# Weight-sum preparation as a second class of side work, and wider steps between its additions

## Chip, cores and metric

The kernel runs on one core of one Trainium2 chip. The metric is the device time of one execution in microseconds (us). The core has a matrix engine (TensorE, PE in the profile; PEld is its weight load), a vector engine (VectorE, DVE), a scalar engine (ScalarE, ACT), a general engine (GpSimd, POOL) and a queue engine that issues most transfers (SyncE, SP). The matrix engine accumulates in PSUM banks; sixteen DMA engines carry all transfers, whichever queue they were issued on.

## What is computed

A trunk of two layers over 256 tokens of width 2048, float32. Each layer adds a token mixer and then a ConvGLU to the residual `h`:

```
h = x
h = h + mlstm_mixer(rmsnorm(h))      # layer 0: input projections, matrix memory in both directions, output projection
h = h + conv_glu(rmsnorm(h))
h = h + hgrn_mixer(rmsnorm(h))       # layer 1: gated linear recurrence in both directions, output projection
h = h + conv_glu(rmsnorm(h))
out = rmsnorm(h)

conv_glu(x): a, v = split(x @ w_up);  (gelu(conv3(a)) * v) @ w_down        # inner width 5504
```

## The kernel before

**Products.** Every weight is float32 and is split on the chip into a high and a low float32r part: ACT copies it to `wh` (L149), DVE subtracts to `wl` (L150); three products (high x high, high x low, low x high) are added in PSUM. The whole work is one list of chunks that `stream` walks through. A chunk is a matrix of 128 x 16 rows and 256 or 512 columns (`fm` with the features, `tm` with the tokens on the partitions), or a pair (`st`). Its raw weights come in loads of 1 MB into three buffers on SP's queue, in the order of the program (`late`, L375, and `load_raw`, L137); the splitting runs three pieces (of 0.5 MB) ahead of the products (`LOOK`).

**Pairs by seven products.** A pair computes 256 x 1024 outputs as 2 x 2 squares per two row tiles, in PSUM banks `pc`. For some of its units (`SEVEN` for the ConvGLU's down projections, `SEVEN_MIX` for a mixer's output projection) it uses seven products in place of eight, with sums of weight squares: T3 = B12 + B22, T1 = B12 + B11, T2 = B11 + T3, T4 = B21 + T2. At the end of the last such unit `mid` spreads the extra banks over the residual `hm`; its last two steps are `hm` additions on POOL (L562, L563). After the pair `done` adds the four `pc` banks (L568, DVE), and the norm's transposes (L414, PE) and squares (L508, ACT) follow.

**Where the sums come from.** For a mixer's pair DVE makes them on the spot (`combine`, L208). For the down projections of a ConvGLU they are prepared ahead into a DRAM scratch, `tscr`, and loaded with the weights (L199, L200). Of the 30 sums of a layer,

- 14 (`BY_TRANSFERS`) are made by transfers alone: `prepare_by_transfers` starts a `unit` every 28 us (`PERIOD`), not while a pair runs (`held`). A unit copies 1 MB from DRAM to DRAM on SP's queue (L375, `tscr<-in_w_d`); 12 us later POOL issues accumulating transfers (L590) that add 256 KB each: T3 and T1 (`tscr<-in_w_d`), then T2 and then T4 (`tscr<-tscr`), each 9 us behind the one before it. All keep the order of the program on their queue, and POOL waits at each for the data that it needs. The generator is started with the third chunk of layer 0's mixer and with the second of layer 1's.
- 16 are made by DVE during the ConvGLU's up projections (`prepare`): loads into `pwh` and `pwl`, four additions (L620), two stores (L623). It is started with the first up chunk of either half of the ConvGLU and begins 18 us later.

**The planner.** `Side` holds the generators that run beside the products: heads of the mixers, norm transposes, the two kinds of preparation. It has a clock of its own, `now`, that the product loops advance (`tick`: 0.65 for each row tile of an `fm` chunk, so 10.4 a chunk; 1.3 for a `tm` one, so 20.8; 0.65 for each product of a pair). A generator is stepped when its time has come; what it yields is the time until its next step. `until(ready)` steps all generators, due or not, again and again until a value is ready; `drain` does so until no generator is left. So the planner sets where in the program an instruction stands; on each engine the pinned ones keep that place, and the others are placed by the program's own estimate of time.

**The mixer's end.** `mixed` makes a mixer's output projection: chunk `c0` (512 columns), the pair `two` (1024), chunk `c3` (512). At the end of `c0`, `done` calls `side.drain()`, closes the mixer's memory and opens that of the pair. Then come `two`, `c3` and the ConvGLU: 22 up chunks, two pairs, 21 up chunks, two pairs. A pair of the ConvGLU begins, in `split_squares`, with a wait until all of its prepared sums have been issued (`ch.waits`).

Of the kernel before, what the change touches and what calls it, by code (L numbers as in the profile page):

```python
# [53 lines left out]
BY_TRANSFERS = 14  # L54
# [13 lines left out]
def trunk_kernel(ctx, tc, xT, x_d, fg_d, pp_d, cst_d, w_gate, w_first, w_aq, w_ak, w_av, w_ao, w_aout, w_ao2,  # L68
# [18 lines left out]
    def col(name, i):  # L87
        o = OFF[name] + i
        return pp[:, o:o + 1]
# [4 lines left out]

    class Side:
        def __init__(self):
            self.now, self.jobs = 0.0, []

        def push(self, gen):
            self.jobs.append([gen, self.now])  # L100

        def step(self, job):
            try:
                job[1] = self.now + (next(job[0]) or STEP)
            except StopIteration:
                self.jobs.remove(job)

        def tick(self, dt):
            self.now += dt
            for job in list(self.jobs):  # L110
                if job[1] <= self.now:
                    self.step(job)

        def until(self, ready):
            while not ready():
                assert self.jobs
                for job in list(self.jobs):
                    self.step(job)

        def drain(self):  # L120
# [2 lines left out]
    side, held = Side(), []  # L123
# [11 lines left out]
    def load_raw(src, b0, b1, start=nc.sync.dma_start):  # L135
        raw = wpool.tile([P, 2048], F32, tag="raw", bufs=RAW, name="raw")
        start(raw[:, :b1 - b0], src[:, b0:b1])  # L137
        return raw
# [46 lines left out]
    def temporary(pool_, name):  # L185
        return pool_.tile([P, 1536], F32, tag="avc", bufs=TEMP if pool_.name == "ff" else 2, name=name)

    def split_squares(ch, parts):

        units, raws, kept = (ch.nk + 1) // 2, {}, {}  # L190
        side.until(lambda: not ch.waits)

        def raw(u):
            if u not in raws and u < units:
                n = 1536 if u in ch.stored else min(2048, 1024 * ch.nk - 2048 * u)
                raws[u] = load_raw(ch.src, 2048 * u, 2048 * u + n)
                if u in ch.stored:
                    kept[u] = temporary(ch.pool, "T")
                    nc.sync.dma_start(kept[u], ch.stored[u][:, 0:1536])  # L199
                    nc.sync.dma_start(raws[u][:, 1536:2048], ch.stored[u][:, 1536:2048])  # L200
            return raws.get(u)

        def combine(u):
            r, T = raw(u), temporary(ch.pool, "T")
            B11, B22, B21, B12 = (r[:, j * 512:(j + 1) * 512] for j in range(4))
            T2, T3, T4 = (T[:, j * 512:(j + 1) * 512] for j in range(3))
            for x, y, out in ((B12, B22, T3), (B12, B11, B12), (B22, B12, T2), (B21, T2, T4)):
                dve.tensor_tensor(out, x, y, ALU.add)  # L208
            kept[u] = T

        for u in range(units):
            r = raw(u)
            yield *parts(r[:, 0:1024], 1024, more=ch.pool), 1
            if u + 1 in ch.seven and u + 1 not in ch.stored:
                combine(u + 1)
            if u in ch.seven:
                yield *parts(kept[u][:, 0:1024], 1024, more=ch.pool), 1
            if 2 * u + 1 < ch.nk:
                yield *parts(r[:, 1024:2048], 1024, more=ch.pool), 1
            if u in ch.seven:  # L220
                yield *parts(kept[u][:, 1024:1536], 512, more=ch.pool), 1
# [152 lines left out]
    def late(dst, src):  # L374
        tc.keep_in_program_order(nc.sync.dma_start(dst, src))  # L375
# [206 lines left out]
    def prepare_by_transfers(todo):  # L582

        def unit(src, dst, left):
            late(dst, src)
            T2, T3, T4, T1 = (dst[:, j * 512:(j + 1) * 512] for j in range(4))
            B11, B12 = src[:, 0:512], src[:, 1536:2048]
            yield 12.0
            for out, in_ in ((T3, B12), (T1, B11), (T2, T3), (T4, T2)):
                tc.keep_in_program_order(pool.dma_start(out, in_, accum_op=ALU.add))  # L590
                if out is not T3:
                    yield 9.0
            left.pop()

        for job in todo:
            while held:
                yield 1.0
            side.push(unit(*job))
            yield PERIOD

    def prepare(mp, todo, period):
# [534 lines left out]
    def ffn(layer, norm, nxt):  # L1136
        stack = ExitStack()
        box = dict(n=STORED * layer)
        chunks, pairs, todo = [], [], []

        def begin():
            box["mp"] = stack.enter_context(tc.tile_pool(name="ff", bufs=1))
            box["mp"].tile([P, LEAD], F32, name="lead")
            for ch in pairs:
                ch.pool = box["mp"]
            if isinstance(nxt, FinalNorm):
                nxt.begin(box["mp"])

        def done_up(f, i, GT, SX, seven):
            def go(ps):  # L1150
                mp, R = box["mp"], norm.R
                avc = temporary(mp, "avc")
                a, v, c = (avc[:, j * T:(j + 1) * T] for j in range(3))
                for z, p in ((a, ps[0]), (v, ps[1])):
                    act.copy(z, p[:, T:2 * T])  # L1155
                    dve.tensor_tensor(z, p[:, 0:T], z, ALU.add)  # L1156
                av = avc[:, 0:2 * T].rearrange("p (a b) -> p a b", a=2)
                dve.tensor_tensor(av, av, R.unsqueeze(1).broadcast_to([P, 2, T]), ALU.mult)
                cw = [col("conv_w", (layer * 3 + w) * FT + f) for w in range(3)]
                act.activation(c, a, AF.Identity, bias=col("conv_b", layer * FT + f), scale=cw[1])  # L1160
                dve.scalar_tensor_tensor(c[:, 1:T], a[:, 0:T - 1], cw[0], c[:, 1:T], ALU.mult, ALU.add)
                dve.scalar_tensor_tensor(c[:, 0:T - 1], a[:, 1:T], cw[2], c[:, 0:T - 1], ALU.mult, ALU.add)
                act.activation(c, c, AF.Gelu)
                dve.tensor_tensor(c, c, v, ALU.mult)
                g = slot(i, "g", mp)
                act.copy(g[:, 0:T], c)
                dve.tensor_tensor(g[:, T:2 * T], c, g[:, 0:T].bitcast(F32), ALU.subtract)
                GT.append(g)
                if i % 2 and i // 2 in seven:
                    n = seven.index(i // 2)  # L1170
                    z = GT[i - 1][:, P:T], GT[i - 1][:, T + P:2 * T]
                    SX[i // 2] = token_sums(mp, n, box["c"], c, avc[:, 0:2 * T], z)
                box["c"] = c
            return go

        for part, (f0, nf) in enumerate(((0, FA), (FA, FB))):
            GT, SX, seven = [], {}, SEVEN[part]

            def prep(part=part, nf=nf):
                if part == 0:  # L1180
                    begin()
                jobs = todo[BY_TRANSFERS:][0:FIRST] if part == 0 else todo[BY_TRANSFERS + FIRST:]
                side.push(prepare(box["mp"], jobs, (nf * 10.4 - 26.0) / len(jobs)))

            for i in range(nf):
                chunks.append(Chunk("fm", w_up[layer, f0 + i], KT, norm.x, done_up(f0 + i, i, GT, SX, seven),
                                    prep if i == 0 else None,
                                    swap=(2,) if part and i == 0 else (3,) if f0 + i == 1 else (), paced=True))

            for c0, src in ((0, w_d0[layer][:, f0 * 1024:(f0 + nf) * 1024]), (2, w_d1[layer][:, f0 * 1024:(f0 + nf) * 1024])):  # L1190
                ch = pair(src, nf, c0, lambda k, GT=GT: GT[k], lambda u, SX=SX: SX[u], nxt if part else None, seven)
                ch.waits = []
                for u in seven:
                    if u != FLY:
                        ch.stored[u] = tscr[box["n"]]
                        ch.waits.append(True)
                        todo.append((src[:, 2048 * u:2048 * (u + 1)], tscr[box["n"]], ch.waits))
                        box["n"] += 1
                pairs.append(ch)
                chunks.append(ch)  # L1200
            if part and isinstance(nxt, FinalNorm):
                pairs[-2].before = nxt.load
                pairs[-1].bank = nxt.bank
        return chunks, stack.close, lambda: side.push(prepare_by_transfers(todo[:BY_TRANSFERS]))


    pool.memset(ones, 1.0)
# [8 lines left out]
    nf = FinalNorm()  # L1216
    chunks = mlstm(n0, n1)
# [111 lines left out]
```

## Time and profile before

| | |
|---|---|
| median of 3 runs | 2431.85 us (2425.56 to 2431.94) |
| profiled execution | 2423.3 us, span 2421.5 us |
| granted TensorE clock in it | 0.992 |
| busy: PE, DVE, ACT, POOL | 98%, 83%, 57%, 12% of the span |
| instructions | 38387 |
| DMA | 624.32 MB, mean 258 GB/s |
| q1 (issued by SP) | 588.49 MB, 69.2% of the DMA engines' time |
| q0 (issued by POOL) | 32.58 MB, 8.9% |

Layer 0's mixer runs to about 424 us, its ConvGLU to about 1118, layer 1's mixer to about 1715, its ConvGLU to the end. The profile gives for each engine how long it was busy; a row of 40 digits shows the busy tenths of 40 slices of 60.5 us. A wait is given as "engine line <- releaser: us in total, times, longest". Durations and waits are from one execution.

### The profile page before, as it was taken

What the parts mean: (1) busy time and instruction counts of PE and PEld (TensorE: products, weight loads), DVE (VectorE), ACT (ScalarE), POOL (GpSimd) and SP (SyncE); (2) the same over time, 40 slices, a digit from 0 to 9 for tenths busy, and PEclk for the clock granted to TensorE, in tenths of its full rate; (3) what the DMA queues carried; (4) which work ended last, traced back from release to release, by engine and by line L of the source; (5) the groups of instructions that cost most, each with busy time, mean ns of one, the idle gap of its engine ahead of it and who ended that gap; (6) DMA issues with size and microseconds to landing.
All of it is one profiled execution on the core that took longest, in us unless ns stands there. A gap on an engine that the chain in (4) does not pass through costs nothing.

```text
span 2421.5 us, 38387 instructions
## 1 busy us (share of the span) xinstructions
PE 2372.3 (98%) x14524; PEld 2022.9 (84%) x14524; DVE 2002.2 (83%) x3244; ACT 1392.3 (57%) x2201; POOL 291.8 (12%) x356
## 2 busy tenths in 40 slices
PE   9999987999999999999999999999999999999998
PEld 8888866888888888887888888888888888888876
DVE  7766656888889888897888888889788889888888
ACT  7655534555566555576555555555655567555565
POOL 0211022000000000000343434330000000000000
PEclk9999988999999999999999999999999999999999
DMA  8986898787788877786787877865778788777785
GB/s 301 268 245 227 253 264 224 269 278 269 268 335 278 279 257 252 245 322 227 224 244 212 244 229 231 238 199 191 240 270 275 265 301 333 275 257 257 248 319 200
DMA packets 123275, 624.32 MB, mean 258 GB/s; under 512 B 13889, under 2 KB 14401, under 8 KB 74705
## 3 DMA queue, kind: packets, MB, share of 16 engines
q1 hardware_dynamic: 105264, 588.49, 69.2%
q0 software_dynamic: 17248, 32.58, 8.9%
q8 instruction: 114, 1.87, 0.3%
q10 hardware_dynamic: 576, 0.79, 0.1%
q14 instruction: 73, 0.59, 0.1%
HBM read 586.09 MB, written 94.44 MB: 281 GB/s over the span
## 4 chain that ended last, share of the span: by engine, by line
PE 84%; DMA 6%; DVE 5%; issue 2%; POOL 1%; ACT 1%; SPq 0%; POOLq 0%; DVEq 0%; ACTq 0%
PE mm L337 35%; PE mm L341 18%; PE mm L353 11%; PE pc L236 10%; PE mm L236 7%; DMA tscr<-in_w_d 3%; DVE wl L150 2%; DMA tscr<-tscr 2%; DVE kq L1015 1%; DMA T<-tscr 1%; PE pn L816 1%; DMA raw<-in_w_d 1%; PE py L1073 1%; DVE QK L1035 1%; DVE QK L1036 0%
## 5 line engine op out<-in xcount | busy, mean ns | idle before, releaser
L337 PE MATMUL mm<-xt,wh 128*128 128x512 f32 x3776 | 1320.5, 396 | 3.5 <-DVE xt L360 3.1
L149 ACT CAST wh<-raw 128x1024 fp32r<-128x1024 f32 (+1 forms) x844 | 875.9, 1043 | 657.9 <-PE mm L337 380.4
L150 DVE TENSOR_TENSOR wl<-raw,wh 128x1024 fp32r<-128x1024 f32 (+1 forms) x844 | 1032.9, 1228 | 260.0 <-ACT wh L149 257.0
L341 PE MATMUL mm<-xt,wl 128*128 128x256 f32 x3776 | 1048.6, 279 | 0.0
L337 PEld LDWEIGHTS mm<-xt,wh 128*128 128x128 f32 x3776 | 706.8, 188 | 166.4 <-DVE xt L360 3.7
L341 PEld LDWEIGHTS mm<-xt,wl 128*128 128x128 f32 x3776 | 710.9, 188 | 4.5 <-issue 0.4
L353 PE MATMUL mm<-wh,xt 128*128 128x512 f32 x1024 | 320.3, 391 | 1.0 <-ACT xt L359 0.8
L236 PE MATMUL pc<-wh,g 128*128 128x512 f32 x696 | 238.0, 390 | 0.0
L353 PEld LDWEIGHTS mm<-wh,xt 128*128 128x128 f32 x1024 | 191.8, 188 | 40.8 <-ACT xt L359 1.3
L353 PE MATMUL mm<-wl,xt 128*128 128x512 f32 x512 | 198.7, 392 | 0.4 <-DVE wl L150 0.4
L236 PE MATMUL mm<-wh,sx 128*128 128x512 f32 x444 | 158.0, 392 | 0.5 <-ACT wh L149 0.5
L562 POOL TENSOR_TENSOR hm<-hm,u 128x512 f32<-128x512 f32 x10 | 15.1, 1505 | 1176.0 <-DVE u L561 1176.0
L236 PEld LDWEIGHTS pc<-wh,g 128*128 128x128 f32 x696 | 131.1, 188 | 27.5
L150 DVE TENSOR_TENSOR wl<-T,wh 128x1024 fp32r<-128x1024 f32 (+1 forms) x148 | 141.4, 966 | 13.4 <-ACT wh L149 13.1
L149 ACT CAST wh<-T 128x1024 fp32r<-128x1024 f32 (+1 forms) x148 | 122.5, 835 | 51.2 <-DMA T<-tscr 14.4
L236 PE MATMUL pc<-wl,g 128*128 128x512 f32 x348 | 135.7, 390 | 0.0
L1155 ACT COPY avc<-mm 128x256 f32<-128x256 f32 x172 | 64.1, 373 | 88.1 <-PE mm L341 88.1
L353 PEld LDWEIGHTS mm<-wl,xt 128*128 128x128 f32 x512 | 96.1, 188 | 20.2 <-DVE wl L150 1.2
L236 PEld LDWEIGHTS mm<-wh,sx 128*128 128x128 f32 x444 | 83.9, 189 | 18.3 <-ACT wh L149 0.9
L236 PE MATMUL mm<-wl,sx 128*128 128x512 f32 x222 | 87.3, 393 | 0.6 <-DVE wl L150 0.6
L1156 DVE TENSOR_TENSOR avc<-mm,avc 128x256 f32<-128x256 f32 x172 | 72.1, 419 | 13.9 <-ACT avc L1155 13.7
L1015 DVE COPY kq<-QK 128x256 f32<-128x256 f32 x224 | 76.4, 361 | 4.2 <-POOL QK L988 4.2
(241 smaller groups left out, 2435.1 us busy)
## 6 DMA issues: line engine op xcount, KB each, us to landing
raw<-in_w_up SPq DMA_DIRECT2D x172, 1024.0 KB, 5.1
raw<-in_w_bq SPq DMA_DIRECT2D x48, 1024.0 KB, 6.5
raw<-in_w_d SPq DMA_DIRECT2D x60, 768.0 KB, 5.7
T<-tscr SPq DMA_DIRECT2D x60, 768.0 KB, 7.3
tscr<-in_w_d SPq DMA_DIRECT2D x28, 1024.0 KB, 9.9
raw<-in_w_ao SPq DMA_DIRECT2D x24, 1024.0 KB, 8.5
raw<-in_w_d SPq DMA_DIRECT2D x24, 1024.0 KB, 6.8
pwh<-in_w_d SPq DMA_DIRECT2D x36, 512.0 KB, 6.5
```

The lines of the kernel that those rows point to most:

```text
L149: pin(act.copy(wh[:, :m], r))
L150: pin(dve.tensor_tensor(wl[:, :m], r, wh[:, :m].bitcast(F32), ALU.subtract))
L236: pe.matmul(ps, a, b, start=id(ps) not in begun, stop=stop and i == 2)
L337: pe.matmul(ps[f], wh[:, c:c + P], x, start=k + kk == 0, stop=False)
L341: pe.matmul(ps[f][:, 0:T], wl[:, c:c + P], x[:, 0:T], start=False, stop=k + kk == ch.nk - 1)
L353: pe.matmul(ps[t], x[:, a + t * P:a + (t + 1) * P], w[:, c], start=st and i == 0, stop=sp and i == 2)
L816: pe.matmul(pn[:, 0:258], w, v, start=(i == 0), stop=(i == len(parts) - 1))
L1015: dve.tensor_copy(m[:, j].rearrange("k (m p j) -> k m p j", p=2, j=h), blocks(z, h, 0, T))
L1035: dve.tensor_tensor(ka, ka, gview(G, n, 1, h), ALU.mult)
L1073: pe.matmul(py[:, c], AT[:, s if s == t else 2 + s], V[:, s, j * P:(j + 1) * P], start=(s == 0), stop=(s == 1))
L1155: act.copy(z, p[:, T:2 * T])
L1156: dve.tensor_tensor(z, p[:, 0:T], z, ALU.add)
```

## The change

`Side` gets a second list, `behind`. The two kinds of preparation are pushed there. `tick` steps both lists, as before; `until` steps the second one only where its new argument says so, which is the wait for a pair's prepared sums. `drain` goes on until the first list is empty and leaves the second one as it is. And a unit's later additions (T2 behind T3 and T1, T4 behind T2) stand 14 in place of 9 apart.

```diff
     class Side:
         def __init__(self):
-            self.now, self.jobs = 0.0, []
-
-        def push(self, gen):
-            self.jobs.append([gen, self.now])
+            self.now, self.jobs, self.behind = 0.0, [], []
+
+        def push(self, gen, behind=False):
+            (self.behind if behind else self.jobs).append([gen, self.now])
 
         def step(self, job):
             try:
                 job[1] = self.now + (next(job[0]) or STEP)
             except StopIteration:
-                self.jobs.remove(job)
+                (self.jobs if job in self.jobs else self.behind).remove(job)
 
         def tick(self, dt):
             self.now += dt
-            for job in list(self.jobs):
+            for job in self.jobs + self.behind:
                 if job[1] <= self.now:
                     self.step(job)
 
-        def until(self, ready):
+        def until(self, ready, behind=False):
             while not ready():
-                assert self.jobs
-                for job in list(self.jobs):
+                them = self.jobs + self.behind if behind else list(self.jobs)
+                assert them
+                for job in them:
                     self.step(job)
 
         def drain(self):
...
     def split_squares(ch, parts):
 
         units, raws, kept = (ch.nk + 1) // 2, {}, {}
-        side.until(lambda: not ch.waits)
+        side.until(lambda: not ch.waits, True)
...
             for out, in_ in ((T3, B12), (T1, B11), (T2, T3), (T4, T2)):
                 tc.keep_in_program_order(pool.dma_start(out, in_, accum_op=ALU.add))
                 if out is not T3:
-                    yield 9.0
+                    yield 14.0
             left.pop()
 
         for job in todo:
             while held:
                 yield 1.0
-            side.push(unit(*job))
+            side.push(unit(*job), True)
             yield PERIOD
...
-                side.push(prepare(box["mp"], jobs, (nf * 10.4 - 26.0) / len(jobs)))
+                side.push(prepare(box["mp"], jobs, (nf * 10.4 - 26.0) / len(jobs)), True)
...
-        return chunks, stack.close, lambda: side.push(prepare_by_transfers(todo[:BY_TRANSFERS]))
+        return chunks, stack.close, lambda: side.push(prepare_by_transfers(todo[:BY_TRANSFERS]), True)
```

## The prediction

> **What bounds the kernel now.** I read the page first: which engine is full, and where it is not.
>
> ```profile
> span 2421.5 us, 38387 instructions
> PE 2372.3 (98%) x14524; PEld 2022.9 (84%) x14524; DVE 2002.2 (83%) x3244; ACT 1392.3 (57%) x2201; POOL 291.8 (12%) x356
> PE   9999987999999999999999999999999999999998
> POOL 0211022000000000000343434330000000000000
> PEclk9999988999999999999999999999999999999999
> ```
>
> TensorE is busy for 2372 of 2421.5 us. The two digits under 9 in mid-row (slices 6 and 7, about 303 to 424 us) are the only place where more than a little can be won; the clock row dips there too, and POOL, nearly idle elsewhere in layer 0, has two 2s. So next the table of stretches (columns: stretch, length, busy time and count of PE, PEld, DVE, ACT, POOL, then granted clock, DMA share, GB/s), first by stage.
>
> ```profile
> 0.00:300.00 300.00, 296.61 (x1706) 251.25 (x1707) 207.37 (x377) 178.09 (x298) 39.30 (x65) 1.00 0.82 257
> 300.00:424.00 124.00, 99.92 (x424) 79.39 (x423) 75.35 (x117) 53.45 (x83) 27.07 (x32) 0.89 0.92 248
> 424.00:660.00 236.00, 236.00 (x1367) 206.50 (x1366) 200.70 (x327) 134.90 (x216) 0.71 (x1) 1.00 0.79 269
> 1126.00:1624.00 498.00, 494.17 (x4439) 424.03 (x4439) 430.11 (x871) 266.97 (x509) 186.23 (x230) 1.00 0.75 223
> 1648.00:1716.00 68.00, 68.00 (x314) 56.40 (x313) 62.05 (x91) 39.95 (x60) 3.54 (x2) 1.00 0.56 195
> ```
>
> 300 to 424 us is the end of layer 0's mixer (its output projection). PE is idle there for 124.0 - 99.9 = 24.1 us, half of all its idle time. The row 1648 to 1716 is the same code in layer 1 (`mixed` builds the same chunks): no idle time, clock 1.00. In finer steps:
>
> ```profile
> 330.00:340.00 10.00, 6.50 (x29) 5.07 (x27) 0.00 (x0) 0.00 (x0) 0.00 (x0) 1.00 1.01 262
> 340.00:350.00 10.00, 3.25 (x6) 1.63 (x6) 6.12 (x12) 4.06 (x4) 0.81 (x1) 0.51 0.92 276
> 390.00:400.00 10.00, 5.46 (x29) 4.21 (x27) 1.14 (x2) 1.05 (x1) 3.34 (x4) 0.91 1.05 293
> 400.00:410.00 10.00, 4.58 (x18) 3.87 (x19) 4.54 (x6) 4.07 (x10) 4.95 (x5) 0.57 0.65 98
> ```
>
> Two holes, and the waits of 296 to 470 us name what ended them, the SP and POOL rows in order of time what stood in front.
>
> ```profile
> DVE T L208 <- DMA raw<-in_w_ao: 18.8, 2, 15.9
> DVE hm L568 <- POOL hm L562: 13.5, 1, 13.5
> 266.80 0.50 SPq L375 DMA_DIRECT2D tscr<-in_w_d  x1
> 298.07 0.50 SPq L375 DMA_DIRECT2D tscr<-in_w_d  x1
> 311.08 3.37 SPq L375 DMA_DIRECT2D tscr<-in_w_d  x5
> 307.04 1.70 POOL L590 DMA_DIRECT2D tscr<-in_w_d  x2
> 402.54 0.81 POOL L590 DMA_DIRECT2D tscr<-tscr  x1 [0.20 <-issue]
> 403.09 1.55 POOL L562 TENSOR_TENSOR hm<-hm,u 128x512 f32<-128x512 f32 x1
> ```
>
> First hole: five copies of 1 MB go to SP's queue in one go, the projection's own weights (`raw<-in_w_ao`) stand behind them, and the splitting of weights waits 15.9 us. Second hole: POOL works through the additions of seven units from 307 to 403 us, each waiting for the one before to land; the residual additions L562 and L563 stand behind them, DVE L568 behind those (13.5 us), and the transposes behind that. Both come from one call: `side.drain()` in `mixed.done` steps every job until none is left, so the units that are not due yet are issued back to back.
>
> **The change part by part.** *What the drain still issues.* On the planner's clock (0.65 a matmul pair of an fm step, 1.3 of a tm step: 10.4 a fm chunk, 20.8 a tm chunk) the transfers begin with the third chunk, at 31.2, one unit every 28; `mixed.done` comes at 4 x 62.4 + 20.8 = 270.4. Units 0 to 8 are out by then (the last at about 256), units 9 to 13 are not: the row x5 above. With the change the drain steps the first class alone, which is empty there, so these five leave the stretch. Unit 8 keeps its three steps: first additions at 268, then 282 and 296. In `two` (270.4 to 310) no unit begins, because `held` is set; unit 9 starts at 311, units 10 to 13 at 339, 367, 395 and 423, and the last addition falls at 463. ConvGLU begins at 331 and its pairs after 22 chunks, at 560, far behind 463: the wait in `split_squares` finds every unit done and costs nothing.
>
> *The gain.* The stretch from `two`'s first product to ConvGLU's first, in layer 0 and in layer 1:
>
> ```profile
> 325.46 0.39 PE L236 MATMUL pc<-wh,ya 128*128 128x512 f32 x1
> 423.71 0.39 PE L337 MATMUL mm<-xt,wh 128*128 128x512 f32 x1
> 1648.02 0.39 PE L236 MATMUL pc<-wh,yb 128*128 128x512 f32 x1
> 1715.40 0.39 PE L337 MATMUL mm<-xt,wh 128*128 128x512 f32 x1
> ```
>
> 98.25 against 67.38 us: 30.9 us for the same products, 24 of idle time and the rest a lower clock behind it. I take all of it as gain. What is late next: POOL still has units 7 and 8 in front of L562, beginning at 307 (row above), six steps with some 7 us to each landing (6.0 and 7.2, rows below): over before 350, while L562 falls due near 360, in the last third of `two`. DMA adds unit 8's additions, the end of unit 7's and the start of unit 9 (16 us of work by the prices below) to the twin's share of 0.56 in 67 us: about 0.80, which ConvGLU bears (0.79) without idle time.
>
> *The price: the five units land in ConvGLU.* What a unit takes of the 16 DMA engines stands in the DMA view of 1126 to 1624 us (layer 1's mixer), and what ConvGLU takes already in that of 440 to 640:
>
> ```profile
> q1 hardware_dynamic: 13166, 95.94, 54.6%
> q0 software_dynamic: 7918, 14.42, 20.4%
> tscr<-in_w_d POOLq DMA_DIRECT2D x28, 256.0 KB, 7.2
> tscr<-tscr POOLq DMA_DIRECT2D x27, 256.0 KB, 6.0
> q1 hardware_dynamic: 9792, 54.53, 79.7%
> ```
>
> q0 is the additions: 20.4% of 498 us over 55 of them is 1.85 us each, 7.4 us a unit. q1: 54.6% of 498 us for 95.94 MB is 2.83 us a MB, 3.0 for a unit's copy. `prepare` begins 18 after ConvGLU, at 349; from there to 463 are 114 of the planner's us, 122 on the chip by the rows below (5.54 us a load, two loads a chunk of 10.4). Free on the engines: 20.3% of 122 = 24.8 us. Wanted: three copies (9.0) and the additions of four units (29.6). The excess is 13.8 us.
>
> ```profile
> L375 SPq DMA_DIRECT2D raw<-in_w_up x37: 327/328/333, 439.7 to 639.3; - x37
>   PE mm L337: 64.5, 51
> DMA to landing us min/median/max: 4.7/5.5/8.5
> ```
>
> Not all of it reaches TensorE. Three raw buffers, 36 x 5.54 us: a load is issued when a buffer comes free and used two loads later, 11.1 us, and it lands after 5.5, so 5.6 us are spare; ACT's casts wait for TensorE (64.5 us, 51 times), so split pieces of 2.8 us each are ready ahead, two of them safely. Cover 11 us. I take 13.8 - 11 = 3 us; the ends are 0 (cover holds, or engines do more than share 1.00, as 1.05 above) and 14. If the cover were gone, it costs the 14.
>
> By bytes it looks milder: ConvGLU's 274 GB/s (54.73 MB in 200 us) and a unit's 2.1 MB in 30 us (28 on the planner's clock) come to 344 GB/s. The Trainium skill, DMA: Bandwidth & Descriptors, section "Where 436 GB/s comes from", puts a core's limit at HBM at about 358 GB/s; by that rule nothing would be in excess and the term would be 0. The trace disagrees for these transfers: the additions take 101.6 us for 14.42 MB.
>
> *9 to 14 between additions, and `until` without the second class.* In layer 1 POOL waits for the additions' landings while its mixer's products stand behind them; wider steps should remove most of that:
>
> ```profile
> POOL tscr L590 <- DMA tscr<-in_w_d: 22.5, 9, 4.0
> POOL tscr L590 <- DMA tscr<-tscr: 13.6, 6, 5.0
> ```
>
> But TensorE is idle only 3.8 us of those 498, so at most that is won, and POOL order may shift as much the other way: -3.8 to +3.8, taken as 0. Layer 1's last unit starts at 10.4 + 364 of 437 and its last addition is at 415, ahead of the mixer's end. In layer 0's first 300 us TensorE misses 3.4 us, the start included: 0, with the same bounds. Other `until` calls find their values ready by the planner's times (R at 27 against 31, the last head's transposes at 257 against 265), so not stepping the second class there changes nothing. No instruction is added or removed.
>
> *Sum.* -30.9 + 3 + 0 = -28 us against the profiled execution's 2423.3 us (span 2421.5): 2395. The three timed runs lie at 2425.56 to 2431.94, median 2431.85, 8.5 above it; taking the same difference there: 2404. About 0.3% (7 us) is what a measurement can tell from no change.
>
> **The rivals.** *Congestion in ConvGLU takes much of it back (0.14).* For: 0.80 + 0.32 is 112% of the DMA engines for 122 us. Against: the cover, and additions that only start when the ones before have landed, so they cannot pile up. Excess fully paid, with fluctuation and some clock: 8 to 22 us back, 2409 to 2423; still faster.
>
> *Slower (0.06).* The same place, but the additions cost double when loads, stores of `prepare` and additions share the engines: 14.8 us a unit makes the excess 43 us, less 11 of cover 32; with the clock lost as in 300 to 424 us (30.9 us of time for 24.1 of idle, 1.28) it is 41 against 31: 10 us slower, 2442. It decides from 1.7 times the price on (12.6 us a unit). Against it: in the densest stretch there is, the price did not rise:
>
> ```profile
> q0 software_dynamic: 4032, 7.34, 38.4%
> ```
>
> That is 300 to 424 us, share 0.92: 47.6 us for seven units, 6.8 each. The clock matters to this rival: after 3.5 us without products (330 to 340) it fell to 0.51. The Trainium skill, TensorE: Matmul & The Clock Gate, section "What's actually happening", says the clock halves after an idle window of about 3.4 us; holes of one missing piece (under 2.8 us) would then cost only themselves, and this case would end level, at 2433, not slower. No row here shows such short holes.
>
> *It does not do what it says (0.07).* The program places POOL's instructions by its own estimate; if the additions of units 7 to 9 still stand in front of L562, or the copies still meet the weights, the holes stay in other sizes: within 7 us of before. Against it: only one unit, not seven, can then be queued.
>
> **How the numbers follow.** Forecast 0.73 (gain 20 to 36 us: 2396 to 2412, with the runs' own spread of 6 us), rivals 0.14, 0.06, 0.07. Faster by over 0.3%: 0.73 + 0.14 = 0.87, less 0.01 for the end of the first rival: 0.86; same 0.08; slower 0.06. The range 2392 to 2420 holds the forecast and most of the first rival.
>
> **What would show it.** In the changed profile: no x5 row on SP near 311 us; L562 starting near 360 us, released by DVE L561; the stretch of 98.25 us at 67 to 70; POOL additions spread to about 530 us; from 400 to 530 us a DMA share near 1.0, and PE's idle time there is the price (3 us here; over 30 means the second rival). PE idle in layer 1's mixer should stay under 8 us. A stretch still over 85 us would make the prediction wrong at its root.

## The result, and the profile after

After the change the kernel takes 2396.86 us (median of 4 runs, 2388.61 to 2399.01) against 2429.87 (2425.56 to 2431.94) before: the ratio is 0.986, with a 95% interval of 0.9832 to 0.9888. Two further sets of runs gave 0.9865 [0.9843, 0.9886] and 0.9842 [0.9822, 0.9863]. It is some 33 us faster; 28 were forecast.

The profiled execution took 2388.61 us. In the new kernel every line from 116 on stands one number higher than before. Its page, the same rows as before:

```profile
span 2386.8 us, 38389 instructions
PE 2364.5 (99%) x14524; PEld 2020.7 (85%) x14524; DVE 2001.0 (84%) x3244; ACT 1392.7 (58%) x2201; POOL 290.9 (12%) x356
PE   9999999999999999999999999999999999999998
POOL 0211011000000000001334333330000000000000
PEclk9999999999999999999999999999999999999999
```

The digits under 9 in slices 6 and 7 are gone from the PE and the clock rows. In layer 1 POOL's digits begin one slice earlier, since layer 1's mixer starts earlier (its first products were at about 1121 us, now at 1095). The table of stretches, with the end of layer 0's mixer first and the start of its ConvGLU behind it:

```profile
300.00:392.00 92.00, 90.33 (x406) 74.10 (x406) 74.12 (x114) 52.36 (x80) 14.06 (x15) 0.98 0.78 232
392.00:660.00 268.00, 267.24 (x1515) 233.74 (x1513) 219.99 (x357) 153.03 (x241) 15.55 (x19) 1.00 0.89 300
400.00:530.00 130.00, 129.24 (x746) 113.24 (x745) 105.45 (x173) 71.93 (x115) 14.02 (x17) 1.00 1.00 331
```

PE is idle for 1.7 us in the first row, where it was 24.1. The DMA engines, which before had a share of 0.79 in ConvGLU, are full from 400 to 530 us, and the matrix engine hardly notices: 0.8 us idle of 130. The first products of `two`, of the last chunk and of ConvGLU, in the timeline:

```profile
325.07 0.39 PE L237 MATMUL pc<-wh,ya 128*128 128x512 f32 x1
370.32 0.62 PE L354 MATMUL mm<-wh,ya 128*128 128x512 f32 x2
394.85 0.39 PE L338 MATMUL mm<-xt,wh 128*128 128x512 f32 x1
```

The stretch is 69.78 us long instead of 98.25: 45.25 in `two` (62.13 before), 24.53 in the last chunk (36.11 before; 24.53 is also its length in layer 1). POOL and SP in order of time, and the wait that is left of the first hole:

```profile
302.38 0.71 POOL L514 TENSOR_TENSOR rs<-rs,mhalf 128x2 f32<-128x2 f32 x1 [42.97 <-DVE rs L513]
338.39 0.81 POOL L591 DMA_DIRECT2D tscr<-tscr  x1 [4.47 <-DMA tscr<-tscr]
371.68 1.29 POOL L563 TENSOR_TENSOR hm<-hm,u 128x512 f32<-128x512 f32 x1 [32.48 <-DVE u L562]
376.27 1.69 POOL L591 DMA_DIRECT2D tscr<-in_w_d  x2 [1.06 <-DMA tscr<-in_w_d]
510.19 0.81 POOL L591 DMA_DIRECT2D tscr<-tscr  x1 [8.80 <-DMA tscr<-tscr]
```

```profile
297.68 0.50 SPq L376 DMA_DIRECT2D tscr<-in_w_d  x1
305.81 45.60 SPq L138 DMA_DIRECT2D raw<-in_w_ao  x8
369.06 0.50 SPq L376 DMA_DIRECT2D tscr<-in_w_d  x1
392.33 0.50 SPq L376 DMA_DIRECT2D tscr<-in_w_d  x1
```

```profile
DVE T L209 <- DMA raw<-in_w_ao: 4.1, 2, 2.6
```

SP goes from a single copy (297.68) to the projection's own weights (305.81); no copy follows until 369. POOL has been idle for 32.48 us when the residual addition L563 (L562 before) comes due, and DVE releases it, not a landing. The last addition is issued at 510.

The whole execution by stages, each the distance between first products in the timeline (start of the program, of `two`, of the last chunk, of ConvGLU, of its first pairs; layer 1's mixer is counted from ConvGLU's last product, and the last pairs up to the end); two more profiled executions of the new kernel and one more of the old one stand beside them:

| stage, us | before | before, 2nd | after | after, 2nd | after, 3rd |
|---|---|---|---|---|---|
| start up to `two`, layer 0 | 325.46 | 327.63 | 325.07 | 326.32 | 331.43 |
| `two`, layer 0 | 62.13 | 63.27 | 45.25 | 47.46 | 46.19 |
| last chunk, layer 0 | 36.11 | 36.97 | 24.53 | 24.53 | 24.53 |
| ConvGLU's first up stage, layer 0 | 245.57 | 245.57 | 246.97 | 253.31 | 251.00 |
| layer 1's mixer up to the output projection | 505.02 | 505.63 | 500.02 | 500.46 | 501.89 |
| last pairs to the end | 120.09 | 116.23 | 116.62 | 118.01 | 116.68 |

In the main profile the stages give -28.5, +1.4, -5.0 and -3.5 us, all others together +0.9: -34.7, the difference of the spans. The -3.5 of the last pairs is not the change's: the second execution of before has 116.23 there as well. The third execution of after begins `two` late, because TensorE once waited 5.39 us near 98 us; E7 below has a like wait.

### The profile page after: what moved, and what is told of

It reads as the page before. It is cut to its first block, busy times and chain, and to the rows that moved or that the text cites. A ratio compares the mean times of both kernels' runs of the same rounds, so it can differ in the third digit from the quotient of the medians.

```text
span 2386.8 us, 38389 instructions
## 1 busy us (share of the span) xinstructions
PE 2364.5 (99%) x14524; PEld 2020.7 (85%) x14524; DVE 2001.0 (84%) x3244; ACT 1392.7 (58%) x2201; POOL 290.9 (12%) x356
## 4 chain that ended last, share of the span: by engine, by line
PE 87%; DMA 5%; DVE 5%; issue 1%; ACT 1%; POOL 0%; SPq 0%; DVEq 0%; POOLq 0%; ACTq 0%
PE mm L338 34%; PE mm L342 17%; PE mm L354 14%; PE pc L237 11%; PE mm L237 7%; DVE wl L151 2%; DMA raw<-in_w_up 1%; DMA T<-tscr 1%; PE pn L817 1%; DMA tscr<-in_w_d 1%; DMA raw<-in_w_ao 1%; PE py L1074 1%; DMA raw<-in_w_d 1%; DMA pwh<-in_w_d 1%; ACT wh L150 0%
## 5 line engine op out<-in xcount | busy, mean ns | idle before, releaser
L563 POOL TENSOR_TENSOR hm<-hm,u 128x512 f32<-128x512 f32 x10 | 15.7, 1566 | 1094.7 <-DVE u L562 1094.7
L237 PEld LDWEIGHTS pc<-wl,g 128*128 128x128 f32 x348 | 65.3, 188 | 13.9 <-DVE wl L151 0.6
```

What stands on the lines that cost most here:

```text
L237: pe.matmul(ps, a, b, start=id(ps) not in begun, stop=stop and i == 2)
L563: pool.tensor_tensor(part(1, 0), part(1, 0), u, ALU.add)
```

## The experiments

Theory: two holes with two causes (copies ahead of the projection's weights on SP; additions ahead of the residual additions on POOL), both out of the one `drain`; the wider spacing is worth nothing. Rivals: the spacing carries the gain, or one cause carries both holes, or the price in ConvGLU is hidden or much larger.

**E1, the spacing alone.** The kernel before, with

```diff
-                    yield 9.0
+                    yield 14.0
```

> The kernel before, with the additions of a unit 14 in place of 9 apart and one class of side work: the drain still issues five units back to back. My theory (the gain is the drain's burst alone): both holes between 300 and 424 us stay, about 98 us from the pair's first product to ConvGLU's first, time within 0.3% of before; layer 1's mixer may be up to 4 us shorter, which is the whole effect of the spacing. Rival (POOL's waits for landings cost time all over, and the spacing takes them away): 10 us or more faster, the second hole smaller.

Ratio 1.0011 [0.9999, 1.0024], 2431.1 against 2428.22 us: no gain. Both holes stay: `two` is 66.24 us long, the last chunk 35.64.

**E2, the classes alone.** The kernel after, with the spacing back:

```diff
-                    yield 14.0
+                    yield 9.0
```

> The changed kernel with the additions 9 apart as before: only the two classes. My theory: the stretch at 68 to 71 us, the whole gain, ratio to before 0.985 to 0.989, layer 1's mixer as before. Rival (spacing shares in it): 0.990 or more, with POOL additions standing in front of the residual additions, or more idle TensorE time in ConvGLU.

0.9891 [0.9873, 0.9909], 2402.04 us. `two` is 44.91, the last chunk 24.53: both holes are gone. The classes carry the gain. Layer 1's mixer is at 505.48, as before. Within the classes only `drain` acts: with `until` stepping both lists, as it did, and `drain` the first alone, the program has the same instructions in the same order on all five engines as E2.

**The kernel after once more,** in the same set:

> The changed kernel as it is, beside the others on one chip. Both theories: ratio 0.983 to 0.989. It shows how much of the 4.3 us that layer 1's mixer and of the 3.5 us that the last pairs were shorter in the first profile comes back: if they do, the spacing has a share; if they do not, they were that execution's.

0.9865 [0.9843, 0.9886], 2399.88 us. Its ratio and E2's overlap, so that the timing alone doesn't tell the spacing from nothing. Of the two differences that it was to show again, that of layer 1's mixer is back in full (500.46), that of the last pairs in part (118.01).

**E4, the second cause taken away by itself.** The kernel before, with the residual additions on DVE, away from POOL's queue:

```diff
-            pool.tensor_tensor(part(1, 0), part(1, 0), u, ALU.add)
-            pool.tensor_tensor(part(1, 1), part(1, 1), u, ALU.subtract)
+            dve.tensor_tensor(part(1, 0), part(1, 0), u, ALU.add)
+            dve.tensor_tensor(part(1, 1), part(1, 1), u, ALU.subtract)
```

> The kernel before, with the last two residual additions of a pair's middle on DVE in place of POOL; the drain and its burst stay. My theory (two holes with two causes, SP's queue and POOL's queue): the second hole (10 us idle and the clock behind it) goes, the first stays; the stretch 84 to 88 us, 10 to 14 us faster, ratio 0.994 to 0.996. Rival (one cause, the DMA engines full of the units): the second hole stays or only moves, within 0.3% of before.

0.9983 [0.9973, 0.9993], 2425.15 against 2428.22 us. The second hole is gone and the first untouched: the last chunk is 24.53, `two` 62.32. So there are two causes. But of the 11.6 us won there the time shows only 3. In the profiles they are lost in ConvGLU, where nothing waits: its first up stage in layer 0 and both up stages in layer 1 take 249.93, 249.93 and 237.55 us instead of 245.57, 245.57 and 233.18, 13.1 us together. The groups of layer 1's first up stage (columns: count, busy, mean ns), in E4 and in before:

```profile
L337 PE MATMUL mm<-xt,wh 128*128 128x512 f32 x683 | 241.4, 399 | 0.0
```

```profile
L337 PE MATMUL mm<-xt,wh 128*128 128x512 f32 x686 | 238.2, 394 | 0.0
```

The same products, no idle time in front of either, and 399 in place of 394 ns for one. As far as the profiles show, the size that E4 was to give failed on this, not on the hole. They are one execution each, and E4's is 3.1 us longer than before's while its median is 3.1 shorter, so that the sizes fit only roughly.

**E5, the first cause put back by itself.** The kernel after, where all copies that are left are issued at the end of the mixer's first output chunk, and the additions keep their new times:

```diff
+        copied = []
+
+        def copy(job):
+            if job not in copied:
+                copied.append(job)
+                late(job[1], job[0])
+
+        rests.append(lambda: [copy(job) for job in todo])
...
+            for rest in rests:
+                rest()
```

> The changed kernel, but at the end of the mixer's first output chunk the copies of all units that have not begun are issued at once on SP's queue (their additions stay spread). My theory (the first hole is SP's queue: five copies of 3 us each in front of the pair's weights): the hole near 340 us is back, the pair 52 to 60 us in place of 45 to 47, no second hole, 7 to 14 us slower than the changed kernel, ratio to before 0.989 to 0.993. Rival (the first hole was the additions' traffic on the DMA engines): the pair at 45 to 48 us, as fast as the changed kernel.

0.9954 [0.9938, 0.9969], 2418.36 against 2429.45 us. SP's row, the wait and the stretches of E5:

```profile
311.54 3.71 SPq L376 DMA_DIRECT2D tscr<-in_w_d  x5
```

```profile
DVE T L209 <- DMA raw<-in_w_ao: 18.0, 2, 17.8
```

```profile
330.00:340.00 10.00, 6.97 (x31) 5.44 (x29) 0.00 (x0) 0.00 (x0) 1.68 (x2) 1.00 1.01 287
340.00:350.00 10.00, 1.37 (x2) 0.79 (x3) 3.72 (x8) 2.09 (x2) 0.81 (x1) 0.55 1.02 294
```

The five copies on SP alone make the whole first hole, 12 us without products at the same place as before; `two` is 61.30 against 42.85 in layer 1, the last chunk stays at 24.53. It is the larger of the two holes: of the 33 us, E5 leaves 11. That is 22 us lost, and not the 7 to 14 expected. `two` is 14 to 16 us longer than in the three executions of the kernel after. The profiled execution (2410.18 us) was the fastest of nine, 8 us under their median, so that no profile shows where the rest goes.

**E6, the price in ConvGLU.** The kernel after, with the last five units not before ConvGLU and twice as close:

```diff
-        for job in todo:
-            while held:
+        for k, job in enumerate(todo):
+            while held or (k >= 9 and side.now < 350.0):
                 yield 1.0
             side.push(unit(*job), True)
-            yield PERIOD
+            yield 14.0 if 349.0 < side.now < 600.0 else PERIOD
```

> The changed kernel, but layer 0's last five units begin only when ConvGLU's own preparation has begun (350 on the planner's clock) and then 14 apart: five units of 10.4 us of DMA time in 103 us of which 21 are free. By my arithmetic the excess is 31 us, less 11 of cover: 20 us slower than the changed kernel, ConvGLU's first up stage about 265 us, ratio to before about 0.994 to 0.996. Rival (the DMA engines or the cover have more room than I gave them): less than 8 us slower, ratio 0.987 to 0.990.

0.9907 [0.9881, 0.9933], 2407.14 us. ConvGLU's first up stage takes 255.99 us, 10.4 over before. One stretch of E6, then the landings of the weights' loads from 440 to 520 us in E6, then those in after:

```profile
440.00:520.00 80.00, 73.39 (x404) 62.27 (x403) 59.10 (x97) 39.58 (x64) 12.81 (x16) 0.98 1.04 339
```

```profile
DMA to landing us min/median/max: 7.3/14.6/18.8
```

```profile
DMA to landing us min/median/max: 6.7/10.1/16.5
```

Here the cover of 11.1 us between a load's issue and its use is over (median 14.6), and PE stands idle for 6.6 of 80 us. In the kernel after, the median lies just under it. A price exists and grows with the density, but less steeply than the excess that I had worked out: the dense case loses 10, not 20. The ratio lies between what my theory and what its rival gave.

**E7 and E8, where the units before the drain go.** The kernel after, with units 18 or 22 apart (in place of 28) in the first 300 us of the planner's clock, so that fewer are left for later:

```diff
-            yield PERIOD
+            yield 18.0 if side.now < 300.0 else PERIOD
```

```diff
-            yield PERIOD
+            yield 22.0 if side.now < 300.0 else PERIOD
```

> The changed kernel with units 18 in place of 28 apart in layer 0's mixer, so that all 14 begin before its first output chunk ends and none is left for ConvGLU. My theory: POOL has the additions of four units between the last heads' scales (306 us) and the residual additions, some eight landings of 7 us, to about 365 us, just when those fall due, and DMA has 40 us of work in the pair on top of its own 0.56: the pair 48 to 56 us, ConvGLU's first up stage at 245.6 us; 0 to 8 us slower than the changed kernel. Rival (what ConvGLU pays is the larger part): 2 to 5 us faster than the changed kernel.

> The changed kernel with units 22 apart in layer 0's mixer: eleven begin there, three are left for ConvGLU, and POOL has two units between the scales and the residual additions as in the changed kernel. My theory: the pair at 45 to 47 us as there, ConvGLU's first up stage free of stalls: 0 to 4 us faster than the changed kernel, ratio to before 0.984 to 0.987. Rival (the mixer's heads wait behind more additions on POOL): slower than the changed kernel, with idle TensorE time before 300 us.

E7: 0.9892 [0.9872, 0.9913], 2403.68 us. ConvGLU's first stage is free of any price (245.57), but `two` takes 51.50: more additions now fall due while POOL waits in front of `two`, they are issued from 315 to 354 us, and the projection's weights come late again. One copy on SP's queue (319.21 us) also stands between the projection's loads. `two` begins late, too, at 333.59 us: 5.65 us of that is one wait of TensorE at 97.7 us, and since the third execution of after has a like one, it isn't shown to belong to E7. A wait and the hole in PE's timeline of E7:

```profile
DVE T L209 <- DMA raw<-in_w_ao: 8.1, 2, 4.2
```

```profile
363.08 0.80 PE L237 MATMUL pc<-wh,ya 128*128 128x512 f32 x1 [5.75 <-ACT wh L150]
```

E8: 0.9849 [0.9826, 0.9872], 2392.99 us; `two` is 44.00, ConvGLU's first stage 246.32. Run again beside the kernel after:

> The changed kernel with units 22 apart in layer 0's mixer, again, beside the changed kernel on the same chip. If moving two units out of ConvGLU is worth what the profiles show (1 us in the pair, 1 to 7 in ConvGLU's first up stage): 2 to 6 us faster than the changed kernel. If not: within 1 us.

> The changed kernel once more, beside the two others of this call: ratio to before 0.984 to 0.989. A third profile of it: ConvGLU's first up stage is 246 to 254 us, at either pace.

E8 0.9839 [0.9819, 0.9859], 2394.6 us; after 0.9842 [0.9822, 0.9863], 2393.3. The two aren't told apart, although `two` is 2.3 us shorter in E8 (43.90 against 46.19). And with only three units left for it, ConvGLU's first up stage takes 253.92 us in E8's second execution, with one stall of TensorE:

```profile
PE mm L342 <- DVE wl L151: 2.4, 1, 2.4
```

So the theory that this stage is free of stalls with three units failed there. No version here is shown to beat the changed kernel.

**E9, the residual additions on DVE in the kernel after** (the edit of E4): the second hole isn't there any more, so what E4 lost should stand alone.

> The changed kernel with the last two residual additions of a pair's middle on DVE, as in the fourth experiment; here nothing stands in front of them on POOL. It asks where that experiment's 11.6 us in the mixer's end went. If the move itself costs time elsewhere (DVE in the five pairs, or a slower pace of the matmuls in ConvGLU): 6 to 10 us slower than the changed kernel. If what was lost there hung on the drain that was still in that kernel: within 3 us of the changed kernel.

0.9876 [0.9858, 0.9893], 2404.02 us, 10.7 above the kernel after beside it (2393.3). Layer 1's up stages are at 249.93 and 237.55 again; the first of them in E9 (after has 394 ns here, as before has):

```profile
L338 PE MATMUL mm<-xt,wh 128*128 128x512 f32 x683 | 241.4, 399 | 0.0
```

By the profiles, of one execution each, the slower products of these two stages make 8.7 us, most of the 10.7 that the medians show. Why they are slower stays open.

**The kernel before once more,** for its stages (second column of the table above):

> The kernel before, a second profile. Both theories: the two holes again, the stretch 95 to 102 us. If the pace of the matmuls in ConvGLU belongs to the execution and not to the program: at least one up stage that took 245.6 us (or 232.8) in the first profile takes some 4.4 us more here, or the reverse.

One execution, 2424.66 us. The holes and layer 1's mixer repeat within 1.2 us; the last pairs don't (116.23 against 120.09). No up stage changed its pace (245.57 again), so this execution doesn't show that the pace belongs to the execution.

## Why the prediction was right, step by step

**The gain, 30.9 us: right, 26.3 to 30.5 measured.** From before's 98.25 and 100.24 the stretch goes to 69.78, 71.99 and 70.72, not quite to the twin's 67.38. E5 and E4 show the two causes one by one. The remainder lies in `two`. The waits of the rows above point to a reason: POOL stood for 43 us, up to 302.38, at a small operation (L514) that had been placed early, and the additions that were due meanwhile came out behind it, between 306 and 339 us, in the middle of `two`, where the loads `raw<-in_w_ao` then landed late (4.1 us). I had counted only unit 8 and parts of 7 and 9 as DMA work there, and thought them spread; they came in a bunch. That POOL order delays other POOL work was in the prediction; that it delays the DMAs themselves was not. E7 (fourteen additions from 315 to 354 us in place of nine, `two` at 51.50) and E8 (nine, but the last at 332 instead of 338 us; `two` at 43.90 to 44.00) fit this; no run takes the bunch away by itself.

**L562 near 360 us: the time was off, the order right.** Its successor L563 starts at 371.68, behind the last products of `two`, not in its last third; DVE releases it, as forecast, with POOL idle for 32 us before.

**The price of 3 us in ConvGLU: the size held within its ends, the mechanism only in part, and partly by luck.** The three executions of after give 1.4, 7.7 and 5.4 us over the 245.57 of before. But the second and the third run this stage's products at 399 ns, the main one at 391 (last section), and with 399 ns the same stage takes 249.93 us in E1 and E4, where no unit is left for it and nothing waits. Against that, the second and third pay 3.4 and 1.1 us. The queue shares from 400 to 530 us in after:

```profile
q1 hardware_dynamic: 6768, 38.12, 78.7%
q0 software_dynamic: 2592, 4.72, 21.2%
```

4.72 MB are 18 additions of 256 KB; 21.2% of 130 us over them is 1.53 us each, below the 1.85 of layer 1. So the rival that needed 1.7 times the price of layer 1 had nothing to stand on. With 1.53 my own sum gives 9.0 + 16 x 1.53 = 33.5 us wanted, an excess of 8.7, less than the cover of 11: a price of 0 (an estimate). Two errors offset one another, an addition priced too high and a cover taken too wide.

The cover gave way in two ways. In the main execution it is the load of my sum, ConvGLU's own weights, that came late; ACT's cast waited for it up to 7.1 us, and TensorE, behind that, 0.8 us:

```profile
ACT wh L150 <- DMA raw<-in_w_up: 17.4, 9, 7.1
```

In the second and third it is another load, which my sum did not have: in its turn DVE waits for `prepare`'s own weights, and the split pieces for TensorE queue up behind that on DVE. The second execution of after shows it in the chain of waits, and its stretches show the hole:

```profile
425.68 9.58 DMA pwl<-in_w_d
435.34 0.69 DVE pwl L621
437.03 1.15 DVE wl L151
438.22 0.39 PE mm L342
```

```profile
430.00:440.00 10.00, 8.05 (x45) 6.83 (x44) 6.96 (x11) 4.36 (x7) 0.00 (x0) 0.95 1.03 400
440.00:450.00 10.00, 10.00 (x52) 8.62 (x52) 9.19 (x16) 6.30 (x11) 1.66 (x2) 0.88 0.98 326
```

A side load of 9.58 us holds up DVE, DVE's next piece `wl` is late, and PE misses 1.95 us. My cover counted the main weights' buffers only. By the page of the Trainium skill that I cited, DMA: Bandwidth & Descriptors, section "Where 436 GB/s comes from", a demand under 358 GB/s would have cost nothing. It did cost a little, with the engines' share at 1.00 and 331 GB/s, and single stretches of 10 us reached 400 GB/s (row above): the share of the engines, not the bytes, was the better warning here. But a share of 1.00 doesn't cost by itself. E2, with the same units at the old spacing, has no idle time there in its one execution:

```profile
400.00:530.00 130.00, 130.00 (x744) 113.10 (x744) 105.82 (x176) 72.64 (x116) 14.71 (x18) 1.00 1.00 331
```

**The spacing taken as 0: layer 1's mixer came out 3 to 5 us shorter, at or past the end of my bounds.** Layer 1's mixer, its first 8.7 us and the rest, in before and then in after:

```profile
1117.30:1126.00 8.70, 5.32 (x29) 3.56 (x28) 8.00 (x25) 7.92 (x19) 1.11 (x1) 0.96 0.79 301
1126.00:1622.30 496.30, 492.47 (x4431) 422.62 (x4431) 428.40 (x863) 266.96 (x508) 186.23 (x230) 1.00 0.75 222
```

```profile
1090.30:1099.00 8.70, 5.33 (x28) 3.51 (x27) 8.08 (x26) 7.92 (x19) 1.19 (x1) 0.95 0.78 300
1099.00:1590.30 491.30, 490.60 (x4432) 422.64 (x4431) 430.06 (x866) 267.40 (x508) 184.33 (x230) 1.00 0.76 225
```

The start is the same. Behind it PE's idle time falls from 3.83 to 0.70 us, nearly all that I had said could be won, and the same products are busy for 1.9 us less, which the bound by idle time left out: 5.0 together. I took the middle of -3.8 to +3.8 without a reason for the loss; the waits for landings that I had quoted spoke for the gain. In the profiles this goes with the spacing within the changed kernel: 505.48 with 9 (E2), 500.02 to 501.93 in each of the nine with 14. In the kernel before, the spacing alone (E1) has 503.97, only 1 us less, and 2.7 us of idle time. So the saving in the profiles is the spacing's only together with the classes; why E1 doesn't have it stays open, with one execution of it. By time the spacing isn't told from nothing (E1; E2 against after).

**The clock behind short holes: my reading failed.** I argued that holes of one piece would cost only themselves, and that no row shows such holes. The trace of before has one, of 2.55 us:

```profile
2355.84 0.50 PE L236 MATMUL mm<-wh,g 128*128 128x512 f32 x1 [2.55 <-ACT wh L149]
```

```profile
2350.00:2360.00 10.00, 6.89 (x25) 4.94 (x24) 7.86 (x8) 6.46 (x9) 4.40 (x2) 0.88 0.76 279
2360.00:2370.00 10.00, 10.00 (x44) 8.24 (x43) 8.65 (x14) 6.12 (x11) 0.00 (x0) 0.95 0.72 234
```

The clock that is missing there, 0.12 and 0.05 of 10 us, is 3.4 us at half speed (0.17 x 10 / 0.5). The hole that is left in after, of 1.67 us:

```profile
349.80 0.73 PE L237 MATMUL mm<-wh,sx 128*128 128x512 f32 x2 [1.67 <-ACT wh L150]
```

```profile
340.00:350.00 10.00, 8.33 (x37) 6.59 (x36) 7.37 (x15) 3.60 (x5) 0.00 (x0) 1.00 0.53 152
350.00:360.00 10.00, 10.00 (x37) 7.84 (x37) 10.00 (x12) 5.84 (x7) 0.00 (x0) 0.83 0.59 200
```

The clock of 0.83 behind it is again 3.4 us at half speed. The hole of 1.95 us in the second execution goes with 0.05 and 0.12 missing, the same once more. In the third execution, 1.19 us of idle time left it at 1.00:

```profile
440.00:450.00 10.00, 8.81 (x51) 7.59 (x51) 9.93 (x16) 6.42 (x11) 1.65 (x2) 1.00 1.01 393
```

Nor does the length of the hole decide. E6 has one of 3.47 us at the same place of the program, and its clock stays at 1.00 in the stretch that holds the hole and in the next:

```profile
352.55 0.73 PE L237 MATMUL mm<-wh,sx 128*128 128x512 f32 x2 [3.47 <-ACT wh L150]
```

```profile
350.00:360.00 10.00, 7.00 (x28) 5.08 (x29) 9.87 (x12) 7.04 (x8) 0.00 (x0) 1.00 0.32 108
360.00:370.00 10.00, 10.00 (x46) 8.28 (x45) 9.26 (x12) 5.44 (x6) 0.00 (x0) 1.00 0.83 303
```

The Trainium skill, TensorE: Matmul & The Clock Gate, section "What's actually happening", lets the clock halve after an idle window of about 3.4 us. The length of the slow spell agrees with that window; as a bound on the idle time it fails here, since 1.67 us was enough and 3.47 us was not. What else decides stays open. Since few such holes came, the sum hardly felt it.

**The sum.** Forecast -30.9 + 3 + 0 = -28; by the stages of the main profile -28.5 + 1.4 - 5.0, and -3.5 that belongs to the execution. The forecast of 2404 lies 7 us above the 2396.86 measured, 3 to 5 of them from layer 1's mixer. The three sets put the gain at 28 to 41 us, which is how far the runs spread.

## What to carry to other kernels

A wait that steps a planner's jobs until all are done issues also those that nobody needs yet, and in-order queues (SP's, POOL's) then make them a barrier for the work behind: drain only what the next step reads, and let the rest keep its dates. Before moving load into a stage with full DMA engines, look at every load that each in-order engine waits for there, the side work's own included. And bound a gain by the idle time of the whole stage, its products' own pace included.

## What was not expected of the hardware

- Long runs of the same products go at one of two paces. ConvGLU's first up stage in layer 0, 450 to 650 us, in after and then in its second execution:

```profile
L338 PE MATMUL mm<-xt,wh 128*128 128x512 f32 x550 | 190.9, 391 | 0.0
```

```profile
L338 PE MATMUL mm<-xt,wh 128*128 128x512 f32 x567 | 200.4, 399 | 0.0
```

With a clock of 1.00 and no idle time one stage takes 245.57 or 249.93 us, the next 233.18 or 237.55. In layer 0 the pace differs between executions of one kernel: after's third is at 399 ns too, E8's first at 391 and its second at 399. In layer 1 both up stages are slow in E4 and E9, the first alone in E1, none elsewhere. What sets it stays open; one profile each doesn't show that moving two additions to DVE is the cause.
- Idle times of 1.67, 1.95 and 2.55 us on TensorE went with 3.4 us at half clock; 1.19 us did not, and neither did 3.47 us in E6. The length of a hole alone doesn't tell.
